# Chunked opening of a two-layer transformer trunk: x and the first weights by 128 contraction rows, bias lines made later and sent by GpSimd

## The chip, the cores and the metric

One of the eight cores of a Trainium2 chip runs the kernel. The metric is the device time of one execution in microseconds; the median of several runs is compared. A profiled execution gives the trace from which all rows here are taken. Engines: PE is TensorE (products), DVE is VectorE, ACT is ScalarE, POOL is GpSimd, SP is SyncE, which only issues DMAs here. ACT and POOL issue DMAs too.

## The reference

```python
# x: (1, 256, 1024) float32; one self layer, one cross layer
def diff_attention(x, w_in, lam_p, subln_g, w_out, rel_bias, lam_init):
    qkv = x @ w_in                      # 1024 -> 1024 Q, 1024 K, 1024 V
    ...                                 # 8 heads of two maps, dh 64, dv 128
    s = einsum('bqhmd,bkhmd->bhmqk', q_blk, k) + rel_bias[rel_bucket(rel)]
    p = softmax(where(rel >= 0, s, -inf))
    a = p[:, :, 0] - lam * p[:, :, 1]
    o = rms_norm(a @ v) * subln_g * (1 - lam_init)
    return o @ w_out

def reference(x, ...):
    h = layer_norm(ALPHA * x + diff_attention(x, ...))
    h = layer_norm(ALPHA * h + square(relu(h @ w_up[0])) @ w_down[0])
    h = layer_norm(ALPHA * h + moba_attention(h, w_q_b, w_out_b, shared_kv(h), rel_bias))
    return layer_norm(ALPHA * h + square(relu(h @ w_up[1])) @ w_down[1])
```

All of it is float32. The logits of both layers get a bias from one table of 32 buckets by 16 heads, chosen by the distance of query and key.

## The kernel before, in words

Every product of a projection is made as three passes: both operands are split into a float32r part (hi) and the rest (lo), and hi*hi, hi*lo and lo*hi accumulate in PSUM. `split_to` does this for a block: ACT copies the hi part, VectorE subtracts it to get lo.

The weights come in 96 units of 1 MB, in the order of their use. A unit is loaded in two pieces of 512 KB (`fetch`, on SP's queue) into five buffers named `raw`; `head` makes a piece's hi half on ACT, `piece` its lo half on VectorE, and then issues the load of the piece five further on, which needs that buffer. `bg` calls `piece` between products, by a credit that products earn. The split halves stand in seven buffers `whi` and `wlo`. From `attention(0, 0)` on every engine runs its instructions in the order of the program; each queue is in order, and a DMA issue that has to wait holds up all that is behind it on its engine. [...]

The opening is written out apart. The transposed x arrives in four parts of 256 KB (two chunks of 128 contraction rows each, all 256 tokens), and with each part two blocks of 256 KB of the first two units. `v_first(u)` (L377) handles a unit of V's first half of columns in two steps j of two chunks: split x (`split_x`), split the weights, the hi*hi products of both chunks and both halves of the tokens, then the lo products. After the first hi*hi products `make_lines` (L186) multiplies the table by a one-hot matrix, which gives one line of 384 biases per head; VectorE copies the lines out of PSUM. Products are 128 rows by 512 columns; V's accumulate in two PSUM banks over the eight chunks. `warm` is a bank for products of zeros ahead of the first real one.

`copy_lines` (L190) writes lines to DRAM (`scr`), 32 copies of each, by one DMA: heads 0 to 3 after `v_first(0)`, heads 4 to 15 after the first `bg`. Both are on ACT's queue. `load_bias` (L194) reads tiles of 128 queries by 256 keys back with four DMAs on SP's queue; the first pair's reads wait for the first copy, the second copy waits for those reads, and the second pair's reads (at i = 2 of the loop) wait for the second copy.

After V's first half, the loop over i (L616) projects Q and K of one pair of heads per round (`project`, 48 products of 256 columns), makes the halves of the pair before (`halves_hi` on ACT, `halves_lo` on VectorE), runs the softmax of the one before that, and multiplies the scores (`scores`, L478 to L480: first q hi by k hi, then q hi by k lo). `make_lambda` comes at i = 1; its two loads are on GpSimd's queue, which has had little else ahead of them.

Of the kernel before, what the change touches and what calls it, by code (L numbers as in the profile page):

```python
"""Differential-attention layer, squared-ReLU MLP, MoBA layer, squared-ReLU MLP, on one core.

Every float32 product of the projections runs as three float32r passes: both operands are
split exactly into a float32r part (11 mantissa bits) and the float32r rest, and
hi*hi + hi*lo + lo*hi accumulate in float32 in PSUM.  Scores are made the same way; the
products of the attention maps with V run as plain float32.

The sequence is one MoBA block, so no block lies in any query's past: the gate masks every
selected block, for all inputs, and the cross layer's softmax is over the own block.
"""  # L10
# [10 lines left out]
F32 = mybir.dt.float32  # L21
# [7 lines left out]
P = 128  # L29
D = 1024  # L30
S = 256
DEPTH = 2
NK = D // P
# [20 lines left out]
def trunk(ctx: ExitStack, tc: tile.TileContext, x, xT, units, lam_a, subln, rel_bias,  # L54
# [13 lines left out]
    def split_to(hi, lo, src, scale=None):  # L68
        """hi + lo = scale * src, both float32r."""
# [13 lines left out]
    def fetch(q):  # L83
        """Piece q's load."""
        if q < NU * PER:
            v, s = divmod(q, PER)
            raws[q] = wpool.tile([P, PIECE], F32, name="raw", bufs=RAWS)
            nc.sync.dma_start(raws[q], units[v][:, s * PIECE:(s + 1) * PIECE])

    def head():  # L90
        """The hi half of the next piece."""
# [13 lines left out]
    def piece():  # L105
        """The lo half of the next piece, after the hi half of a later one."""
# [12 lines left out]
    def bg(most=8, force=False):  # L119
        """Pieces of later units, as many as the products since the last ones have room for."""  # L120
# [7 lines left out]
    def unit(u, **dims):  # L128
        """The halves of unit u; units that were used up before are free from here on."""
# [5 lines left out]
    def three(ps, w, a, moving_w, n, start, stop):  # L135
        """ps += the product of a unit's block and an activation's, both (hi, lo)."""
# [29 lines left out]
    for q in range(4):  # L166
        raws[q] = wpool.tile([P, PIECE], F32, name="raw", bufs=RAWS)
        c = slice(q * 512, (q + 1) * 512)
        nc.sync.dma_start(xTr[:, c], xT[:, c])
        for j in range(2):  # L170
            d = (q % 2) * PIECE + j * 512
            nc.sync.dma_start(raws[q][:, j * 512:(j + 1) * 512], units[q // 2][:, d:d + 512])
# [17 lines left out]
    def copy_lines(h0, h1):  # L190
        nc.scalar.dma_start(scr[:, h0:h1].rearrange("p h r -> h p r"),
                            line[h0:h1, None, :].to_broadcast([h1 - h0, COPIES, RELS]))

    def load_bias(layer, p):  # L194
        """The tiles of pair p's two heads."""
# [6 lines left out]
    def split_x(s):  # L202
        k = slice(2 * s, 2 * s + 2)
        src = xTr.rearrange("p (k t) -> p k t", k=NK)[:, k]
        split_to(act[0][:, k], act[1][:, k], src)

# [18 lines left out]
    def rsqrt(v, n, scale=1.0, eps=None, eng=nc.vector, fill=()):  # L225
        """1/sqrt(scale * v + eps) of v [P, n]: a guess from the bits, then two steps.

        The guess is taken at an eighth.  The first step is of the third order,
        y <- y * (15 - 10 z + 3 z * z) / 8 with z = v * y * y, the second one Newton's,
        y <- y * (3 - z) / 2; the factors are shared out so that each is one instruction.  # L230
        `fill`: independent instructions, to be put between the dependent ones."""
# [16 lines left out]
        def shifted(o, a, c, b):  # L248
            """o <- (a + c) * b."""
# [745 lines left out]
```

## Time and profile before

| | us |
|---|---|
| median of three runs | 621.1 |
| lowest, highest | 619.33, 625.88 |
| span of the profiled execution | 621.2 |
| TensorE busy in it | 603.8 |
| VectorE busy | 385.8 |
| ACT busy | 325.5 |
| GpSimd busy | 15.4 |

The span runs from the first to the last instruction of the profiled execution, and is that execution's own time as the profile gives it. Busy time counts an engine's own instructions, and not the issuing of DMAs. In the rows below a timeline line is: start in us, duration in us, engine, line of the code, operation, output<-inputs, shapes, count; in brackets the idle time of the engine before it and what ended that.

### The profile page before, as it was taken

The numbers are of one execution on the slowest core, as the hardware profiler recorded it, in microseconds if no ns is written. First come the engines' busy times: TensorE is split into PE (matmuls) and PEld (weight loads), VectorE is DVE, ScalarE is ACT, GpSimd is POOL, SyncE is SP. The second block draws the span as 40 slices with busy tenths as digits, with TensorE's granted clock in tenths as the row PEclk, the third lists the DMA queues.
The fourth block names the chain that finished last, engine by engine and source line by source line (L and its number), as shares of the span: only waits on it lengthen the run. The fifth ranks groups of instructions, "written<-read, shape, count | busy, mean of one in ns | idle before, by whom it ended". The sixth has DMA issues, their size and how long they took to land.

```text
span 621.2 us, 9556 instructions
## 1 busy us (share of the span) xinstructions
PE 603.8 (97%) x3674; PEld 533.2 (86%) x3674; DVE 385.8 (62%) x706; ACT 325.5 (52%) x556; POOL 15.4 (2%) x40
## 2 busy tenths in 40 slices
PE   8999999999999999999999999999999999999994
PEld 5998987888898899898889899988898898899883
DVE  5479888877634734653877577877767534544236
ACT  5477787447654754552346466462586654554200
POOL 2000011000000000000020000000000000000000
PEclk9999999999999999999999999999999999999998
DMA  8797684547666556556258655341588656553001
GB/s 298 226 312 233 199 257 153 187 169 238 200 222 221 177 197 238 194 178 204 68 165 286 205 157 170 103 143 60 166 303 267 216 179 207 177 181 103 1 0 69
DMA packets 36985, 113.86 MB, mean 183 GB/s; under 512 B 4603, under 2 KB 9756, under 8 KB 36940
## 3 DMA queue, kind: packets, MB, share of 16 engines
q1 hardware_dynamic: 35056, 108.02, 52.9%
q0 software_dynamic: 1264, 4.39, 2.1%
q10 hardware_dynamic: 620, 0.84, 0.4%
q8 instruction: 29, 0.48, 0.3%
q14 instruction: 16, 0.13, 0.1%
HBM read 111.40 MB, written 1.84 MB: 182 GB/s over the span
## 4 chain that ended last, share of the span: by engine, by line
PE 74%; issue 10%; DMA 7%; DVE 5%; ACT 2%; POOL 1%; SPq 0%; DVEq 0%; POOLq 0%; ACTq 0%
PE ps_a L140 11%; PE ps_a L139 11%; PE ps_a L141 11%; PE ps_b L143 9%; PE ps_b L145 9%; PE ps_b L144 9%; DMA raw<-in_units 5%; PE ps_b L141 3%; PE ps_b L139 3%; PE ps_b L140 3%; DVE wlo L113 2%; DMA bias<-scr 1%; ACT whi L101 1%; PE ps_c L288 1%; PE ps_c L533 1%
## 5 line engine op out<-in xcount | busy, mean ns | idle before, releaser
L113 DVE TENSOR_TENSOR wlo<-raw,whi 128x1024 fp32r<-128x1024 f32 x188 | 222.8, 1221 | 66.6 <-ACT whi L101 66.1
L101 ACT ACTIVATE whi<-raw 128x1024 fp32r<-128x1024 f32 x188 | 190.4, 1053 | 83.8 <-PE ps_a L141 49.7
L143 PE MATMUL ps_b<-act_hi,whi 128*128 128x256 f32 x640 | 182.4, 285 | 0.0
L145 PE MATMUL ps_b<-act_hi,wlo 128*128 128x256 f32 x640 | 180.2, 282 | 0.0
L144 PE MATMUL ps_b<-act_lo,whi 128*128 128x256 f32 x640 | 179.9, 281 | 0.0
L144 PEld LDWEIGHTS ps_b<-act_lo,whi 128*128 128x128 f32 x640 | 120.6, 188 | 0.6
L143 PEld LDWEIGHTS ps_b<-act_hi,whi 128*128 128x128 f32 x640 | 120.5, 188 | 0.6
L145 PEld LDWEIGHTS ps_b<-act_hi,wlo 128*128 128x128 f32 x640 | 120.5, 188 | 0.0
L139 PE MATMUL ps_a<-whi,h_hi 128*128 128x512 f32 x248 | 98.5, 397 | 0.0
L141 PE MATMUL ps_a<-whi,h_lo 128*128 128x512 f32 x248 | 98.3, 396 | 0.0
L140 PE MATMUL ps_a<-wlo,h_hi 128*128 128x512 f32 x248 | 98.3, 396 | 0.0
L72 DVE TENSOR_TENSOR h_lo<-sqr,h_hi 128x512 fp32r<-128x512 f32 x24 | 16.6, 692 | 80.5 <-ACT h_hi L70 80.5
L141 PEld LDWEIGHTS ps_a<-whi,h_lo 128*128 128x128 f32 x248 | 46.7, 188 | 11.3
L140 PEld LDWEIGHTS ps_a<-wlo,h_hi 128*128 128x128 f32 x248 | 46.8, 189 | 10.8
L139 PEld LDWEIGHTS ps_a<-whi,h_hi 128*128 128x128 f32 x248 | 46.7, 188 | 10.8
L762 ACT ACTIVATE relu<-ps_b 128x512 f32<-128x512 f32 x32 | 19.1, 596 | 67.1 <-PE ps_b L145 56.8
L500 ACT ACTIVATE t<-t,mx 128x256 f32<-128x256 f32 x64 | 28.4, 444 | 34.5 <-DVE mx L497 34.5
L139 PE MATMUL ps_b<-whi,act_hi 128*128 128x512 f32 x96 | 39.4, 410 | 0.4 <-ACT act_hi L70 0.4
L141 PE MATMUL ps_b<-whi,act_lo 128*128 128x512 f32 x96 | 38.0, 396 | 1.0 <-DVE act_lo L74 1.0
L140 PE MATMUL ps_b<-wlo,act_hi 128*128 128x512 f32 x96 | 37.9, 395 | 0.0
L139 PE MATMUL ps_a<-whi,act_hi 128*128 128x512 f32 x80 | 32.5, 407 | 0.0
L140 PE MATMUL ps_a<-wlo,act_hi 128*128 128x512 f32 x80 | 31.6, 395 | 0.0
(142 smaller groups left out, 628.4 us busy)
## 6 DMA issues: line engine op xcount, KB each, us to landing
raw<-in_units SPq DMA_DIRECT2D x188, 512.0 KB, 5.2
bias<-scr SPq DMA_DIRECT2D x64, 64.0 KB, 4.2
raw<-in_units SPq DMA_DIRECT2D x8, 256.0 KB, 5.3
lnp<-in_ln_g POOLq DMA_DIRECT2D x4, 512.0 KB, 4.3
lnp<-in_ln_b POOLq DMA_DIRECT2D x4, 512.0 KB, 4.9
xres<-in_xT SPq DMA_DIRECT2D x4, 256.0 KB, 5.2
xres<-in_x SPq DMA_DIRECT2D x1, 1024.0 KB
scr<-lnp ACTq DMA_DIRECT2D x1, 576.0 KB
```

Source lines behind the costliest of these rows:

```text
L72: nc.vector.tensor_tensor(lo, src, hi.bitcast(F32), op=ALU.subtract)
L101: nc.scalar.activation(split[v][0][:, c], raws[state["head"]], AF.Copy)
L113: nc.vector.tensor_tensor(split[v][1][:, c], raws.pop(state["piece"]), split[v][0][:, c].bitcast(F32), op=ALU.subtract)
L139: nc.tensor.matmul(ps, a[0], w[0], start=start, stop=False)
L140: nc.tensor.matmul(ps, a[0], w[1], start=False, stop=False)
L141: nc.tensor.matmul(ps, a[1], w[0], start=False, stop=stop)
L143: nc.tensor.matmul(ps, w[0], a[0], start=start, stop=False)
L144: nc.tensor.matmul(ps, w[0], a[1], start=False, stop=False)
L145: nc.tensor.matmul(ps, w[1], a[0], start=False, stop=stop)
L288: nc.tensor.transpose(pt[:, j * P:(j + 1) * P], src[:, j * P:(j + 1) * P], ident)
L500: nc.scalar.activation(t[:, m, s], t[:, m, s], AF.Exp, bias=mx[:, m, j:j + 1], accum_out=sm[:, m, j:j + 1])
L762: nc.scalar.activation(r, ps, AF.Relu)
```

## The change

The x loads become eight of one chunk each, every one followed by the weight block of the same chunk. `v_first` goes by single chunks: split x, split the weights, then hi*hi for both halves of the tokens, lo*hi for both and hi*lo for both. In chunks 0 and 1 a product of zeros of 128 columns stands between the hi*hi and the lo products. `make_lines` moves from behind the first hi*hi products to behind chunk 4. The first copy of the lines moves from between the two V units to behind both, and both copies are issued by GpSimd instead of ACT. Comment lines and docstrings are blank in the new file; from L167 on its lines move by up to three.

```diff
-    for q in range(4):
-        raws[q] = wpool.tile([P, PIECE], F32, name="raw", bufs=RAWS)
-        c = slice(q * 512, (q + 1) * 512)
-        nc.sync.dma_start(xTr[:, c], xT[:, c])
-        for j in range(2):
-            d = (q % 2) * PIECE + j * 512
-            nc.sync.dma_start(raws[q][:, j * 512:(j + 1) * 512], units[q // 2][:, d:d + 512])
+    for k in range(NK):
+        if k % 2 == 0:
+            raws[k // 2] = wpool.tile([P, PIECE], F32, name="raw", bufs=RAWS)
+        nc.sync.dma_start(xTr[:, k * S:(k + 1) * S], xT[:, k * S:(k + 1) * S])
+        nc.sync.dma_start(raws[k // 2][:, (k % 2) * 512:(k % 2 + 1) * 512],
+                          units[k // 4][:, (k % 4) * 512:(k % 4 + 1) * 512])
...
     def copy_lines(h0, h1):
-        nc.scalar.dma_start(scr[:, h0:h1].rearrange("p h r -> h p r"),
+        nc.gpsimd.dma_start(scr[:, h0:h1].rearrange("p h r -> h p r"),
...
-    def split_x(s):
-        k = slice(2 * s, 2 * s + 2)
-        src = xTr.rearrange("p (k t) -> p k t", k=NK)[:, k]
-        split_to(act[0][:, k], act[1][:, k], src)
+    def split_x(k):
+        split_to(act[0][:, k], act[1][:, k], xTr[:, k * S:(k + 1) * S])
...
-                for j in range(2):
-                    q = 2 * u + j
-                    ks = (2 * j, 2 * j + 1)
-                    split_x(q)
-                    for k in ks:
-                        split_to(hi[:, k], lo[:, k], raws[q][:, (k % 2) * 512:(k % 2 + 1) * 512])
-                    del raws[q]
-                    fetch(q + RAWS)
-                    for k in ks:
-                        for h in range(2):
-                            nc.tensor.matmul(pv[0, h], at(4 * u + k, h)[0], hi[:, k], start=u == k == 0, stop=False)
-                    if q == 0:
+                for k in range(4):
+                    q, kk = 2 * u + k // 2, 4 * u + k
+                    split_x(kk)
+                    split_to(hi[:, k], lo[:, k], raws[q][:, (k % 2) * 512:(k % 2 + 1) * 512])
+                    if k % 2:
+                        del raws[q]
+                        fetch(q + RAWS)
+                    a = [at(kk, h) for h in range(2)]
+                    for h in range(2):
+                        nc.tensor.matmul(pv[0, h], a[h][0], hi[:, k], start=kk == 0, stop=False)
+                    if kk < 2:
+                        nc.tensor.matmul(warm[:, :P], zero[:, :P], zero[:, :P], start=True, stop=True)
+                    for h in range(2):
+                        nc.tensor.matmul(pv[0, h], a[h][1], hi[:, k], start=False, stop=False)
+                    for h in range(2):
+                        nc.tensor.matmul(pv[0, h], a[h][0], lo[:, k], start=False, stop=kk == NK - 1)
+                    if kk == 4:
                         make_lines()
-                    for k in ks:
-                        for h in range(2):
-                            a = at(4 * u + k, h)
-                            nc.tensor.matmul(pv[0, h], a[1], hi[:, k], start=False, stop=False)
-                            nc.tensor.matmul(pv[0, h], a[0], lo[:, k], start=False, stop=u == 1 and k == 3)
...
                 v_first(0)
+                v_first(1)
                 copy_lines(0, 4)
-                v_first(1)
                 load_bias(0, 0)
```

## Rows read from the trace of the kernel before

**Rows 1.** The page's part 1: busy us (share of the span) and instructions.

```profile
PE 603.8 (97%) x3674; PEld 533.2 (86%) x3674; DVE 385.8 (62%) x706; ACT 325.5 (52%) x556; POOL 15.4 (2%) x40
```

**Rows 2.** Timeline of ACT and VectorE in the opening.

```profile
5.29 0.63 ACT L70 ACTIVATE whi<-raw 128x512 fp32r<-128x512 f32 x1 [0.32 <-DMA raw<-in_units]
...
9.87 0.55 DVE L188 COPY lnp<-ps_c 16x384 f32<-16x384 f32 x1 [1.98 <-PE ps_c L187]
...
10.45 0.28 ACTq L191 DMA_DIRECT2D scr<-lnp  x1
```

**Rows 3.** Timeline of TensorE in the opening.

```profile
5.98 2.46 PE L395 MATMUL ps_a<-whi,act_hi 128*128 128x512 f32 x4 [0.74 <-ACT whi L70]
8.37 1.46 PE L187 MATMUL ps_c<-lnp,table 33*16 33x384 f32 x2
9.76 0.79 PE L401 MATMUL ps_a<-whi,act_lo 128*128 128x512 f32 x1
...
12.06 0.63 PE L402 MATMUL ps_a<-wlo,act_hi 128*128 128x512 f32 x1
12.49 0.55 PE L401 MATMUL ps_a<-whi,act_lo 128*128 128x512 f32 x1
12.88 0.39 PE L402 MATMUL ps_a<-wlo,act_hi 128*128 128x512 f32 x1
...
21.01 0.40 PE L401 MATMUL ps_a<-whi,act_lo 128*128 128x512 f32 x1
21.24 0.40 PE L402 MATMUL ps_a<-wlo,act_hi 128*128 128x512 f32 x1
```

**Rows 4.** Windows: stretch, its length, busy us (count) by engine; PEclk, DMA share, GB/s.

```profile
4.00:13.00 9.00, 8.23 (x17) 4.16 (x17) 5.21 (x9) 5.99 (x11) 0.87 (x2) 1.00 1.01 355
```

**Rows 5.** Timeline of SP from 20 us on, issues of one line merged.

```profile
21.79 1.75 SPq L198 DMA_DIRECT2D bias<-scr  x4
23.64 13.38 SPq L88 DMA_DIRECT2D raw<-in_units  x8
38.64 1.74 SPq L198 DMA_DIRECT2D bias<-scr  x4
```

**Rows 6.** Waits of SP's queue up to 40 us: total, times, longest.

```profile
SPq L198 <- DMA scr<-lnp: 7.2, 2, 5.6
```

**Rows 7.** One link of the chain; VectorE's timeline at that place.

```profile
24.11 6.92 DMA raw<-in_units
...
23.07 1.23 DVE L113 TENSOR_TENSOR wlo<-raw,whi 128x1024 fp32r<-128x1024 f32 x1 [0.69 <-ACT whi L101]
```

**Rows 8.** Timeline of TensorE and VectorE at 33 and 48 us.

```profile
33.19 0.47 PE L478 MATMUL ps_a<-kz,qh 128*128 128x512 f32 x1
34.42 0.47 PE L479 MATMUL ps_a<-kz,qh 128*128 128x512 f32 x1 [0.76 <-DVE kz L468]
...
47.25 0.42 DVE L491 CUSTOM_DVE_ANT_0 t<-ps_a,bias 128x256 f32<-128x256 f32 x1 [2.33 <-DMA bias<-scr]
...
48.09 0.40 PE L478 MATMUL ps_a<-kz,qh 128*128 128x512 f32 x1
49.80 0.50 PE L479 MATMUL ps_a<-kz,qh 128*128 128x512 f32 x1 [1.31 <-DVE kz L468]
```

**Rows 9.** Bias tiles' landing up to 60 us; DMA issues up to 40 us.

```profile
DMA to landing us min/median/max: 2.2/4.8/6.4
...
lnp<-in_lam_a POOLq DMA_DIRECT2D x1, 128.0 KB, 5.9
ident<-in_ident POOLq DMA_DIRECT2D x1, 64.0 KB, 4.3
```

**Rows 10.** DMA queue of ACT, 14.1 to 21.3: packets, MB, share of 16 engines.

```profile
q10 hardware_dynamic: 131, 0.20, 7.4%
```

**Rows 11.** The same from 31 to 38.7 us.

```profile
q10 hardware_dynamic: 396, 0.59, 25.0%
```

**Rows 12.** Timeline of VectorE: the first instruction that reads lambda's load.

```profile
36.58 0.28 DVE L217 TENSOR_TENSOR lp<-lnp 128x128 f32<-128x128 f32 x1
```

## The prediction

> **What bounds the kernel now.** The page's busy times come first: TensorE is busy for 603.8 of 621.2 us [rows 1]. Past the opening the kernel is a row of products, so a change to the first 22 us can give two things: the time at which that row becomes gapless, and the waits that start-up loads cause a little later. TensorE's timeline has two such waits, at 33 and at 48 us, both for the low halves of keys that VectorE makes; they are read below. Nothing after about 50 us is touched.
>
> The opening is read from the timeline by engine. The first real product starts at 5.98, when ACT has the first weight chunk's high half (5.29 to 5.92) [rows 2, 3]. Four hi*hi products follow with gaps, then the lines' product at 8.37, and from there TensorE has no gap worth naming; the stage's last product starts at 21.24 and ends at 21.64 [rows 3]. [...] The windows view grants 1.00 in all of 4 to 13, so here the spacing has to be read instead [rows 3, 4].
>
> Two in-order queues lose time to the bias lines. VectorE waits 1.98 us for the lines' product before it copies them, and ACT issues their way to DRAM at 10.45 [rows 2]. SP then stands 5.6 us, from 16.2 to 21.79, because its first bias tiles read that copy; weight loads follow only at 23.64 [rows 5, 6].
>
> That hole returns later. The chain shows the load issued at 24.11 as one link of 6.92 us. It would put VectorE's low half ahead of it, but that one starts at 23.07, takes 1.23 us and ends at 24.30, after the issue: what set 24.11 is SP's order behind the bias tiles [rows 7]. The load lands at 31.03; ACT splits it, makes the halves of pair 0 behind it, VectorE the low ones, and TensorE, which started the scores at 33.19, goes on at 34.42 [rows 8]. The wait from 48.09 to 49.80 goes back to bias tiles too: VectorE stands until 47.25 for tiles that SP issued at 38.64 [rows 5, 8].
>
> **Loads in chunks.** The bytes are the same: eight x loads of 128 KB for four of 256 KB, the weights as before. That is four more issues of about 0.44 us on SP (1.75 for four [rows 5]), at most 1.8 us, and it delays the last chunk most; by 355 GB/s [rows 4] 384 KB take 1.1 us, so that chunk lands near 13.5 and TensorE comes to it after 18 (below). I take nothing; without that cover it would be the 1.8. The first weight chunk has 128 KB less in front of it, 0.4 us at that rate. First product: 5.98 - 0.43 = 5.55, at worst 5.98.
>
> **Splitting and products by chunk.** A chunk costs ACT 0.63 for the weights [rows 2] and some 0.35 for x, VectorE about 0.65 and 0.35 (from 1.23 for 1024 columns [rows 7], estimates): 1.0 each, less than the loads' 1.1. [...]
>
> When the clock rises is the disputed cost. It rose 4.5 us after 8.37 and 3.1 us after 9.76, from where the spacing is even; before 8.37 there are gaps of up to 0.74 us [rows 3]. I take 4.5, as 8.37 opens the last stretch without a gap: 10.05. The ends are 3.1 (8.7) and no earlier than now (12.9). [...]
>
> With 10.05: (10.05 - 5.55)/0.43 = 10.5 products are done, 42.5 x 0.232 = 9.9 remain, end 19.9. Then the lines: their product stands behind chunk 4 now, and VectorE's copy of them ahead of chunk 5's low halves. TensorE is through the lines (35 of the 53) at 10.05 + 24.5 x 0.232 = 15.7, the copy (0.55 [rows 2]) ends at 16.3, and chunk 5's products with low halves wait about 0.5 for x and 0.15 for the weights. V ends at 20.55 instead of 21.64: **-1.1 us**, between -1.7 (8.7) and +0.2 (12.9).
>
> VectorE, which would be through chunk 4 near 11, stands until then. Chunks 5 to 7 end on it at 19.3, and the four pieces behind (1.23 each) at 20.6 to 24.3. The first Q/K unit wants its low half at 20.8: just covered. Two weight loads that wait for chunks 5 and 7 issue at 17.3 and 19.4, where the last was out by 16.2; they fall into the hole in the loads.
>
> **The lines' copy on GpSimd.** It is issued at 16.3 instead of 10.45. How long 192 KB take there is not shown. From below: a bias load at its best, 2.2 us [rows 9], so 18.5. From above: as long as on ACT, 10.45 to 21.79 = 11.3, so 27.6. But all of that copy's packets (128 rows) moved in 14.1 to 21.3, for 7.4% of the engines' time [rows 10], among weight loads; at 17 to 20 there are one or two of those. The nearest rows are GpSimd's own loads of 64 and 128 KB, 4.3 and 5.9 us in the crowded opening [rows 9]; I take 4.5: SP is free at 20.8, 1.0 earlier. [...]
>
> The loads behind SP then come 1.0 earlier: 31.03 becomes 30.0. Against that, the second copy (576 KB, waits for the first bias tiles' landing as it did on ACT) starts near 25.5, where on ACT it moved in 31 to 38.7 for 25.0% of the engines' time [rows 11]. A quarter of three us is +0.75. So TensorE resumes at 34.2 instead of 34.42, though it would be ready at 32.3: of the 1.1 us **-0.25 us** is left; the rest goes into a longer wait. Ends: -2.1 (TensorE's own order, copy in 2.2 us) and +5.8.
>
> The second pair's bias tiles wait for the second copy. If that takes 8 us, between 5.9 for 128 KB [rows 9] and the rest of the present one, it lands near 33.5; then SP's own order decides, just after its last load is out, 37.0 - 0.25 = 36.8 instead of 38.64 [rows 5]. Of 1.85 us, 1.5 can be used, since TensorE's wait is 1.71 less a product's 0.23 [rows 8]: **-1.3 us**, bounds 0 (the tiles queue behind weight loads whenever they are issued) and -1.5.
>
> The loads for lambda now queue behind both copies on GpSimd: issued near 26.5, behind the second copy's packets, landing at 33 to 35.5. VectorE wants them at 36.58 [rows 12]. Taken as nothing; each us beyond costs VectorE one.
>
> Sum: -0.25 - 1.3 = -1.55; 621.2 - 1.55 = 619.6. The profiled span, 621.2, stands at the median of the three runs, 621.1.
>
> **Rivals.** *Gain lost* (0.2): the copies on GpSimd bring the bias tiles no earlier, TensorE arrives sooner and waits longer at 33 and 48: 621.2. For it: 34.42 is set by loads, not by products. Against: SP's 5.6 us. If chunks land no sooner than now, that is 0.4 us of V's gain and ends here too.
> *Slower* (0.15): the first copy, made 5.9 us later than now, lands later than now. Its place is SP's queue, where every weight load waits. It decides from 5.5 us on (21.8); with the second copy's gain counted, the kernel is slower from 6.8. With 11.3 us SP is free 5.8 late: 627.0; midway, 8 to 9 us, 623 to 624.
> *Both stages gain* (0.15): clock at 8.7, copies near 2.2 us. V -1.7, the waits of 1.0 and 1.5 gone: -4.2, 617.0.
>
> **How the numbers follow.** Forecast 0.5, alone 618.2 to 620.8. The range runs from the large gain with 0.2 for the spread of its terms, 616.8, to the middle of the slow rival, 623.5; it leaves out some 0.08 on either side. One per cent is 6.2 us, about what a measurement of this kernel can tell from no change. No sum reaches -6.2 but by errors in several terms (0.04); the slow rival reaches +6.2 only at its end with some loss besides (0.05); the rest, 0.91, lies within.
>
> **What would show it.** First V product near 5.55; spacing 0.23 from 8.7 to 12.9 on; VectorE waiting 4 to 5 us for the lines' product, copy done near 16.3; V's end near 20.55; SP's first bias issue near 20.8; TensorE resuming the scores at about 34.2; the second pair's tiles issued near 36.8 and the wait at 48 nearly gone. I am wrong if SP's bias issue comes after 21.8, if GpSimd's copy moves at ACT's pace, or if VectorE's late pieces, not loads, hold TensorE at 20 to 26.

## The result and the profile after

The changed kernel takes 626.4 us (median of 20 runs, 624.43 to 630.04) against 621.83 (20 runs of the kernel before beside them, 618.95 to 625.88). The ratio is 1.0077, interval 1.0059 to 1.0095: 0.8% slower, where a gain of 0.25% was forecast, and outside the range.

The page's part 1 of the changed kernel, as in [rows 1], shows hardly more work on any engine (GpSimd 17.1 us against 15.4); TensorE is busy for 603.4 us against 603.8, in a span of 623.7 against 621.2. The loss is idle time.

```profile
PE 603.4 (97%) x3678; PEld 533.3 (86%) x3678; DVE 386.5 (62%) x710; ACT 325.8 (52%) x560; POOL 17.1 (3%) x42
```

TensorE's timeline of the changed kernel, to be read beside [rows 3] and [rows 8]: the V stage starts at 5.71 and runs at 0.23 us per product nearly from its start (two products take from 6.97 to 7.43), so it is through at 19.30 (18.66 + 0.64), 2.3 us ahead of before. Then come two waits of 3.28 and 0.76 us ahead of the first scores, which end 1.9 us behind before (36.33 against 34.42), and one of 1.69 at the third pair's scores, which ends 4.35 behind (54.15 against 49.80).

```profile
5.71 0.74 PE L391 MATMUL ps_a<-whi,act_hi 128*128 128x512 f32 x2 [0.47 <-ACT whi L70]
...
6.97 0.62 PE L397 MATMUL ps_a<-wlo,act_hi 128*128 128x512 f32 x2
7.43 0.68 PE L391 MATMUL ps_a<-whi,act_hi 128*128 128x512 f32 x2
...
18.66 0.64 PE L397 MATMUL ps_a<-wlo,act_hi 128*128 128x512 f32 x2
...
35.11 0.47 PE L475 MATMUL ps_a<-kz,qh 128*128 128x512 f32 x1 [3.28 <-ACT kz L455]
36.33 0.77 PE L476 MATMUL ps_a<-kz,qh 128*128 128x512 f32 x1 [0.76 <-DVE kz L465]
...
54.15 0.50 PE L476 MATMUL ps_a<-kz,qh 128*128 128x512 f32 x1 [1.69 <-DVE kz L465]
```

Where this comes from is read off four queues. VectorE's timeline has the copy of the lines out of PSUM, the first lambda instruction, and the softmax of the first and the second pair (`t<-ps_a,bias`):

```profile
14.23 0.55 DVE L187 COPY lnp<-ps_c 16x384 f32<-16x384 f32 x1 [2.40 <-PE ps_c L186]
...
41.15 0.29 DVE L214 TENSOR_TENSOR lp<-lnp 128x128 f32<-128x128 f32 x1 [2.57 <-DMA lnp<-in_lam_a]
...
42.28 0.42 DVE L488 CUSTOM_DVE_ANT_0 t<-ps_a,bias 128x256 f32<-128x256 f32 x1
...
51.60 0.43 DVE L488 CUSTOM_DVE_ANT_0 t<-ps_a,bias 128x256 f32<-128x256 f32 x1 [1.90 <-DMA bias<-scr]
```

GpSimd's timeline has the two copies and the lambda load, SP's the bias tiles:

```profile
15.09 0.77 POOL L190 DMA_DIRECT2D scr<-lnp  x1 [11.20 <-DVE lnp L187]
28.91 0.69 POOL L190 DMA_DIRECT2D scr<-lnp  x1 [13.06 <-DMA bias<-scr]
29.60 0.62 POOL L210 DMA_DIRECT2D lnp<-in_lam_a  x1
```

```profile
24.91 1.75 SPq L197 DMA_DIRECT2D bias<-scr  x4
26.76 12.46 SPq L88 DMA_DIRECT2D raw<-in_units  x8
40.52 1.74 SPq L197 DMA_DIRECT2D bias<-scr  x4
```

These rows are one serial chain: lines, first copy, first bias tiles, second copy (its issue waits for those tiles, as the bracket of 28.91 says), second bias tiles, second pair's softmax. Link by link, before [rows 2, 5, 8] and after; the second copy of before is this line of ACT's timeline:

```profile
26.56 0.32 ACTq L191 DMA_DIRECT2D scr<-lnp  x1
```

| step | before | after | link is longer by |
|---|---|---|---|
| lines copied from | 9.87 | 14.23 | +4.36 |
| first copy issued | 10.45 | 15.09 | +0.28 |
| SP issues first bias tiles | 21.79 | 24.91 | -1.52 |
| second copy issued | 26.56 | 28.91 | -0.77 |
| SP issues second bias tiles | 38.64 | 40.52 | -0.47 |
| second pair's softmax starts | 47.25 | 51.60 | +2.47 |

From the lines to that softmax both kernels take 37.4 us, though single links differ by up to 2.5 us and only cancel in the sum. The lines are made 4.36 us later, the softmax comes 4.35 later, and the median is 4.57 later. That coincidence of sums is a reading; the experiments test it.

The two spans differ by less, 2.5 us, but the rest is not made up in the opening. From the second softmax on both kernels run the same instructions on VectorE, and matched one by one the changed kernel is 4.4 us behind still at 145 us. Past that the kernel before waited more in this execution: its last 2900 products take 476.9 us from start to start, the changed kernel's 475.4. This execution lay above its median: in the nineteen other profiled ones the device time is 1.8 to 2.2 us above the span, which puts this one near 623.1, about 1.3 above 621.83 (an estimate from those figures).

### The profile page after: what moved, and what is told of

Read it like the earlier page. It is cut to its first block, busy times and chain, and to the rows that moved or that the text cites. A ratio compares the mean times of both kernels' runs of the same rounds, so it can differ in the third digit from the quotient of the medians.

```text
span 623.7 us, 9580 instructions
## 1 busy us (share of the span) xinstructions
PE 603.4 (97%) x3678; PEld 533.3 (86%) x3678; DVE 386.5 (62%) x710; ACT 325.8 (52%) x560; POOL 17.1 (3%) x42
## 4 chain that ended last, share of the span: by engine, by line
PE 75%; issue 10%; DMA 8%; DVE 4%; ACT 2%; POOL 1%; SPq 1%; DVEq 0%; POOLq 0%; ACTq 0%
PE ps_a L140 11%; PE ps_a L141 11%; PE ps_a L139 11%; PE ps_b L143 9%; PE ps_b L145 9%; PE ps_b L144 9%; PE ps_b L141 3%; PE ps_b L139 3%; PE ps_b L140 3%; DMA raw<-in_units 3%; DMA lnp<-in_lam_a 2%; DVE wlo L113 2%; DMA scr<-lnp 2%; DMA bias<-scr 1%; PE ps_c L285 1%
## 5 line engine op out<-in xcount | busy, mean ns | idle before, releaser
L141 PEld LDWEIGHTS ps_a<-whi,h_lo 128*128 128x128 f32 x248 | 46.7, 188 | 11.3
L140 PEld LDWEIGHTS ps_a<-wlo,h_hi 128*128 128x128 f32 x248 | 46.8, 189 | 10.8
L139 PEld LDWEIGHTS ps_a<-whi,h_hi 128*128 128x128 f32 x248 | 46.7, 188 | 10.8
L141 PE MATMUL ps_a<-whi,act_lo 128*128 128x512 f32 x80 | 31.6, 395 | 0.0
## 6 DMA issues: line engine op xcount, KB each, us to landing
scr<-lnp POOLq DMA_DIRECT2D x1, 576.0 KB, 11.6
```

Source lines behind the costliest of these rows:

```text
L139: nc.tensor.matmul(ps, a[0], w[0], start=start, stop=False)
L140: nc.tensor.matmul(ps, a[0], w[1], start=False, stop=False)
L141: nc.tensor.matmul(ps, a[1], w[0], start=False, stop=stop)
```

## The experiments

All are timed in five rounds beside the kernel before, on its chip. A profile is one execution, and the profiled ones lay up to some 3 us from their kernel's own median, so ratios are taken from all runs and places from the profile.

| kernel | lines | copy 1 | bias 1 | copy 2 | bias 2 | softmax 2 | span | profiled time less median | ratio |
|---|---|---|---|---|---|---|---|---|---|
| before | 9.87 | 10.45 | 21.79 | 26.56 | 38.64 | 47.25 | 621.2 | about +1.3 | 1 |
| after | 14.23 | 15.09 | 24.91 | 28.91 | 40.52 | 51.60 | 623.7 | -0.8 | 1.0077 |
| e1 | 15.38 | 15.96 | 25.20 | 29.03 | 42.46 | 50.28 | 624.4 | 0.0 | 1.0074 |
| e2 | 8.48 | 9.33 | 19.84 | 25.74 | 36.94 | 46.65 | 619.6 | -2.4 | 1.0042 |
| e3 | 14.37 | 14.95 | 24.01 | 28.51 | 39.64 | 48.58 | 624.1 | +1.7 | 1.0051 |
| e4 | 15.08 | 15.93 | 26.08 | 29.57 | 41.88 | 50.50 | 623.5 | -0.2 | 1.0071 |
| e5 | 10.47 | 11.32 | 21.75 | 26.82 | 38.25 | 47.69 | 621.3 | -2.8 | 1.0068 |
| e6 | 15.71 | 16.29 | 25.33 | 28.71 | 40.86 | 49.48 | 624.2 | +1.5 | 1.0039 |
| e7 | 15.19 | 16.05 | 24.04 | 28.00 | 37.73 | 46.76 | 617.3 | -0.9 | 0.9965 |
| e8 | 9.77 | 11.15 | 21.44 | 25.90 | 39.66 | 48.94 | 618.4 | +0.9 | 0.9952 |
| e9 | 10.64 | 11.21 | 21.11 | 28.25 | 38.00 | 50.50 | 625.5 | +2.4 | 1.0069 |
| e10 | 15.60 | 16.45 | 25.81 | 29.71 | 41.39 | 50.62 | 625.2 | +0.3 | 1.0083 |
| e11 | 14.76 | 15.61 | 25.46 | 29.43 | 41.39 | 50.80 | 625.2 | +0.2 | 1.0094 |
| e12 | 12.57 | 13.15 | 23.10 | 27.75 | 39.82 | 48.25 | 620.5 | +0.3 | 0.9989 |
| e13 | 16.51 | 17.36 | 27.19 | 31.09 | 42.61 | 51.85 | 625.3 | +0.2 | 1.0113 |
| e14 | 11.71 | 12.28 | 23.34 | 30.17 | 40.69 | 50.49 | 622.8 | +0.3 | 1.0056 |
| e15 | 16.57 | 17.42 | 27.28 | 31.28 | 42.88 | 54.03 | 626.1 | +1.3 | 1.0089 |
| e16 | 11.98 | 12.56 | 18.56 | 25.72 | 35.79 | 43.50 | 614.5 | -3.0 | 0.9983 |
| e17 | 17.02 | 17.87 | 27.99 | 35.52 | 46.06 | 55.18 | 630.3 | +0.6 | 1.0132 |
| e18 | 12.32 | 12.90 | 18.86 | 28.31 | 37.08 | 47.23 | 620.7 | 0.0 | 1.0027 |

The columns are the steps of the chain above, in us. Over the 20 rows the span goes with the start of the second softmax: correlation 0.90, 1.2 us of span per us (least squares); without the five kernels with spread lines (e7, e8, e12, e16, e18), whose products are quicker all through (below), 0.89 and 0.96. The link to the lines is looser: e6's lines come 5.84 us behind before's, its second softmax 2.23. And the chain has a second end. In eight profiles (e2, e3, e5, e7, e10, e11, e13, e17) the second softmax waits for no bias tile; it follows the first one at 7.2 to 7.5 us, and the first one stood behind the lambda load, for which VectorE waited 0.9 to 8.7 us and which lies behind the second copy on GpSimd. So the second softmax is a good sign of an execution's length; what causes it rests on the edits below that move the chain on purpose.

**e1 to e4: who issues the copies.** e1, e3 and e4 give both copies, the first, or the second of the changed kernel back to ACT; e2 gives both copies of the kernel before to GpSimd.

```diff
     def copy_lines(h0, h1):
-        nc.gpsimd.dma_start(scr[:, h0:h1].rearrange("p h r -> h p r"),
+        nc.scalar.dma_start(scr[:, h0:h1].rearrange("p h r -> h p r"),
```

> The changed kernel with both copies of the lines issued by ACT again; all else as changed. Theory 1 (GpSimd's copies hold SP and share the weight loads' engines): the whole loss goes, SP's first bias issue comes before 22 us although the lines are made near 14.5, and the time is 618.5 to 622 (ratio to before 0.995 to 1.000). Theory 2 (the lines are made too late, whoever sends them): SP is freed no earlier than about 24, and the time stays at 624 to 627.

> The kernel before with both copies issued by GpSimd; loads, products and lines as before. Theory 1: the first copy takes 9 to 10 us from 10.5 and lands near 20 to 22, the second takes 11 to 12 us and slows weight loads and lambda's loads behind it; the time is 1 to 4 us above before (ratio 1.002 to 1.006). Theory 2: the lines are as early as before, so the time is that of before within 0.2 per cent.

> The changed kernel with only the first copy (heads 0 to 3) issued by ACT, the second still by GpSimd. Theory 1, if the first copy's hold on SP is what costs: SP freed before 22, time 619 to 622.5. If the second copy and lambda's loads behind it cost most: 623 to 626. Theory 2: 624 to 627.

> The changed kernel with only the second copy (heads 4 to 15) issued by ACT, the first still by GpSimd. Theory 1 with the first copy as the cause: SP still freed near 25, time 624 to 627. With the second copy as the cause: 619 to 622.5. Theory 2: 624 to 627.

Measured: e1 1.0074 (1.0046 to 1.0103), e3 1.0051 (1.0028 to 1.0073), e4 1.0071 (1.0039 to 1.0103), e2 1.0042 (1.0020 to 1.0064). From its issue to SP's bias issue the first copy takes 9.2 us on ACT in e1 and 9.1 in e3, 10.5 on GpSimd in e2 and 9.8 in the changed kernel. The theory that GpSimd's way of issuing is the cause falls: with ACT the loss stays. e1's queue rows:

```profile
15.96 0.27 ACTq L190 DMA_DIRECT2D scr<-lnp  x1
...
25.20 1.75 SPq L197 DMA_DIRECT2D bias<-scr  x4
```

GpSimd costs something where all else is as before (e2), and there the lambda load lies behind the second copy, so that the first softmax waits for it and starts at 39.42 and not at 37.71; but with the chunks in place its share is not to be told from nothing. VectorE's timeline of e2:

```profile
38.28 0.29 DVE L217 TENSOR_TENSOR lp<-lnp 128x128 f32<-128x128 f32 x1 [4.24 <-DMA lnp<-in_lam_a]
```

**e5, e6, e9, e10: the parts alone and by twos.** e5 is the changed kernel with lines and first copy behind chunk 1; e6 the kernel before with the lines made behind its third step (`if q == 2`) and the first copy behind both V units; e9 the changed kernel with lines early, first copy between the units and ACT issuing, so that only the chunks remain; e10 is e6 with GpSimd issuing.

```diff
 e5, e9:
-                    if kk == 4:
+                    if kk == 1:
                         make_lines()
 e6, e10:
-                    if q == 0:
+                    if q == 2:
                         make_lines()
```

> The changed kernel with the lines made after chunk 1 (not 4) and the first copy issued by GpSimd right behind them. Theory 2 (the copy takes 9 to 11 us from whoever sends it, so what counts is when the lines are made): the copy is issued near 10, SP is freed near 20 to 21, the wait before the first scores shrinks below 1.5 us; time 619 to 622.5 (ratio 0.997 to 1.002). Theory 3 (chunk loads or the products' new order cost the time): it stays at 624 to 627.

> The kernel before, its loads, splits and products by pairs of chunks as before and both copies on ACT, with the lines made behind the hi*hi products of chunks 4 and 5 and the first copy behind both V units. Theory 2: SP is freed 3 to 5 us later than before, near 25 to 27; time 624 to 627. Theory 3: within 0.2 per cent of before.

> The chunks alone: lines made behind chunk 1 and their first copy sent between the two units, both copies by ScalarE as before; only the order of loads, splits and products is the changed kernel's. Theory A (the chunks themselves cost, since the V projection that ends 1 to 2 us earlier is only a longer wait for the weight and bias loads, after which TensorE's clock is halved): ratio 1.002 to 1.004, a wait of over 3 us on TensorE ahead of the first scores and a granted clock near 0.5 behind it. Theory B (the chunks cost nothing by themselves; the late lines and GpSimd's copies are all of it): ratio 0.997 to 1.001, no wait over 3 us.

> The two other parts without the chunks: the kernel before with its lines made behind the first unit's third quarter, the first copy sent behind both units, and both copies by GpSimd. If the late place (+0.39% alone) and GpSimd (+0.42% alone) add up: ratio 1.007 to 1.009, as much as the whole change. If they cost the same thing once (the first copy, 9 to 11 us long by either issuer, lies beside the same weight loads): 1.003 to 1.005, and the chunks' share of the change is the rest, some 0.3 to 0.4%.

Measured: e5 1.0068 (1.0037 to 1.0100), e6 1.0039 (1.0010 to 1.0068), e9 1.0069 (1.0041 to 1.0098), e10 1.0083 (1.0053 to 1.0112). With c for the chunks, l for the late lines and g for GpSimd the eight combinations are, in per cent: none 0, c 0.69, l 0.39, g 0.42, cl 0.74, cg 0.68, lg 0.83, clg 0.77. Without the chunks l and g add up; with them neither adds anything that can be measured. Each part alone makes the kernel slower, and the whole costs no more than the chunks alone, as far as these figures tell (each is uncertain by some 0.3). In e5 and e9 SP issues the first bias tiles at 21.75 and 21.11, no later than before, and the loss is there all the same: the late first copy is one cause and not the only one.

That the chunks cost, though V ends sooner, was the surprise. Neither expectation for e9 was met: the ratio lies above both ranges, and TensorE does not wait ahead of the first scores. In e9's profile V is through at 19.88 (19.25 + 0.63), and TensorE then waits for weights and runs on at half pace, as its timeline shows; in the window from 20 to 25 us the granted clock is 0.73:

```profile
19.25 0.63 PE L397 MATMUL ps_a<-wlo,act_hi 128*128 128x512 f32 x2
20.69 0.39 PE L143 MATMUL ps_b<-act_hi,whi 128*128 128x256 f32 x1 [0.81 <-ACT whi L101]
...
21.95 0.38 PE L145 MATMUL ps_b<-act_hi,wlo 128*128 128x256 f32 x1 [0.76 <-DVE wlo L113]
```

And the first bias tiles, issued at 21.11, free the second copy only at 28.25: 7.1 us, against 4.8 in the kernel before. There the stretch from 20 to 25 us is nearly empty, with 0.31 of the DMA engines busy, since SP has stood behind the copy; here the weight loads that were issued later run in it, at 0.93. The second softmax is at 50.50, 3.25 us behind before. This profile lay 2.4 us above its median, so the size may be too large. That this is how the chunks cost is a reading of one profile, and no edit tests it.

**e14, e13: loads by chunks or products by chunks.** e14 gives the kernel before the 16 loads of the changed kernel and leaves all else; e13 gives the changed kernel the 12 loads of before.

```diff
 e14 (e13 is the reverse, in the changed kernel)
-    for q in range(4):
-        ...
-        nc.sync.dma_start(xTr[:, c], xT[:, c])
+    for k in range(NK):
+        ...
+        nc.sync.dma_start(xTr[:, k * S:(k + 1) * S], xT[:, k * S:(k + 1) * S])
```

> The kernel before with the changed kernel's 16 loads at the start; it splits and multiplies by quarters as before, lines early, copies by ScalarE. Theory L: the load behind the V units starts a us later or more, less moved by 30 us than 7.90 MB, ratio 1.003 to 1.007, most of what the chunks cost alone (1.0069). Theory N, and the theory that it is the product order by chunks that costs: ratio 0.998 to 1.001.

> The changed kernel with x loaded by quarters of two chunks again (12 loads at the start in place of 16); split and multiplied by chunks, late lines and GpSimd as changed. Theory L (16 loads hold the load queue longer, so that the load behind the V units starts 1 us later, 9.85 against 8.89, and 1.1 MB less has been moved by 30 us, which TensorE then waits for): that load starts before 9.0 us, the sum moved by 30 us rises by 0.3 MB or more, ratio 1.002 to 1.006. Theory N (the loads' size doesn't matter; with late lines the first copy and what waits for it is all): ratio 1.007 to 1.009 as changed, and under 7.0 MB by 30 us.

Measured: e14 1.0056 (1.0027 to 1.0085), which looks like most of what the chunks cost. In SP's timeline of e14 the loads of the later units start at 12.77, where before had 8.89 in the same view, and the first bias tiles, issued at 23.34, take 6.8 us until the second copy leaves at 30.17.

```profile
12.13 0.43 SPq L170 DMA_DIRECT2D raw<-in_units  x1
12.77 10.51 SPq L88 DMA_DIRECT2D raw<-in_units  x5
23.34 1.83 SPq L197 DMA_DIRECT2D bias<-scr  x4
```

But the loads are not alone in that delay. e14 splits x by pairs of chunks, so its first split waits for the second chunk of x, which now comes behind the first weights. In this kernel alone ACT's table load, 1.28 us long and through by 3.6 us in all the others, stands behind that wait. The first V product starts at 8.21 (before: 5.98), and V ends 3.2 us behind before's. ACT's and TensorE's timelines of e14:

```profile
5.71 1.28 ACT L70 ACT_TABLE_LOAD   x1 [5.71 <-DMA xres<-in_xT]
...
8.21 2.07 PE L394 MATMUL ps_a<-whi,act_hi 128*128 128x512 f32 x4 [2.97 <-ACT whi L70]
```

So its 0.56% is not the price of the loads alone.

e13 came out the other way than that theory asked: 1.0113 (1.0070 to 1.0155), no better than the changed kernel, though its later loads start at 8.32. Its lines come at 16.51, 2.3 us behind the changed kernel's, because VectorE waits 4.54 us for their product behind chunk 4, and the chain ends at 51.85. TensorE went through the first chunks at half pace in that execution (the two products at 7.16 take 1.20 us, where the changed kernel's take 0.71), so part of these 2.3 us may be its clock's. No run shows that loads by chunks cost anything where the splits go by chunks too: with loads by quarters e13 is no faster than the changed kernel, and e16 (below) no faster than e12.

**e7, e8, e12: lines spread over more partitions.** The first copy reads four lines, which lie on partitions 0 to 3. Theory 4 is that the copies are paced by the partitions that they read from. Here head h's line stands on partition 4h; a table of 64 columns, used in every fourth, puts it there. Everything else is as changed (e7), as before (e8), or as in e9 (e12).

```diff
-    table = const.tile([NBUCKET + 1, NH], F32, name="table")
+    table = const.tile([NBUCKET + 1, 4 * NH], F32, name="table")
...
-    nc.scalar.dma_start(table[:NBUCKET], rel_bias)
+    nc.scalar.dma_start(table[:NBUCKET, ::4], rel_bias)
...
-                            line[h0:h1, None, :].to_broadcast([h1 - h0, COPIES, RELS]))
+                            line[4 * h0:4 * h1:4, None, :].to_broadcast([h1 - h0, COPIES, RELS]))
```

> The changed kernel with the line of head h on partition 4h instead of h (the one-hot product makes 64 rows, three of four unused); bytes, packets, issuers and order as changed. [...] If the count of DMA engines or the writing to DRAM sets the pace: SP freed near 25, time 624 to 627.

> The kernel before with the line of head h on partition 4h; all else as before. Theory 4: the first copy, issued near 10.5 on ACT, lands by 17 instead of 21.8, SP no longer waits for it longer than for its own buffers, and the waits at 33 and 48 shrink; time 617 to 620.5. If not: that of before within 0.2 per cent.

> The chunks with lines early, copies by ScalarE, and the lines of the 16 heads on every fourth partition. Theory 4 (the copies are paced by the partitions that they read from): second copy under 9.5 us, lambda loads landed a us or two earlier; ratio 0.993 to 0.998, no slower than the spread lines with the changed order (0.9965). If the chunks cost what theory A says, it stays above the kernel before with spread lines (0.9952); if they cost nothing, it is the fastest of all, 0.993 to 0.995.

Measured: e7 0.9965 (0.9933 to 0.9996), e8 0.9952 (0.9922 to 0.9982), e12 0.9989 (0.9956 to 1.0022). The same edit takes 1.1% off the changed kernel and 0.8% off e9; e7 and e8 are faster than the kernel before, the only ones whose interval says so, though e7's lines are as late as ever. The copies fell short of theory 4, though: e7's still takes 8.0 us, against 9.8 in the changed kernel, and e8's is through at 21.44 and not by 17. That e8's time fell into the expected range is in part luck, as follows. The DMA view by queue, from 15 to 25 us of the changed kernel and from 16 to 24.1 of e7 (packets, MB, share of 16 engines), shows the first copy as q0 with the same packets and bytes:

```profile
q1 hardware_dynamic: 556, 2.00, 51.6%
q0 software_dynamic: 192, 0.20, 16.3%
```

```profile
q1 hardware_dynamic: 673, 2.41, 75.4%
q0 software_dynamic: 192, 0.20, 6.9%
```

0.163 x 16 x 10 us is 26 us of engine time in the one, 0.069 x 16 x 8.1 is 9 us in the other; the weights beside it move faster too. In the kernel before [rows 10], where the copy went out earlier among more weight loads, its packets took 0.074 x 16 x 7.2 = 8.5 us, no more than spread ones. The lines' copy takes 8.0 us in place of 9.8 and the second 9.7 in place of 11.6 (issue to the next issue), and the second softmax moves from 51.60 to 46.76, ahead of before, and waits for no bias tile:

```profile
46.76 0.42 DVE L488 CUSTOM_DVE_ANT_0 t<-ps_a,bias 128x256 f32<-128x256 f32 x1
```

In e8 the chain shows no gain: the copies take 10.3 and 13.8 us there, and the second softmax, at 48.94, waits 4.84 us for the bias, more than before. What made e8 faster lies outside the opening: matched by VectorE's instructions it is 3.6 us behind before at 145 us still, and its span is 2.8 us shorter. In all five kernels with spread lines TensorE's products follow each other more quickly through the whole kernel: the last 2900 of them, counted from start to start without gaps over 0.5 us, take 469.1 to 470.8 us, where the fifteen others need 473.4 to 474.0 (before 473.6, e8 470.3, e7 470.8). A product of 256 columns comes every 117 ns there and every 119 elsewhere (medians). Part 1 of the pages of e8 and e7, to be read beside [rows 1]:

```profile
PE 598.3 (97%) x3674; PEld 530.8 (86%) x3674; DVE 386.6 (63%) x706; ACT 326.0 (53%) x556; POOL 15.4 (2%) x40
```

```profile
PE 598.7 (97%) x3678; PEld 531.1 (86%) x3678; DVE 386.7 (63%) x710; ACT 325.4 (53%) x560; POOL 17.0 (3%) x42
```

For e8 that is 3.3 us, as much as its whole gain of 0.48%; for e7 it is 2.8 us, 0.45%. No wait in the opening explains it. The edit also makes `table` four times as wide, and no run has that alone, so its cause is open. What is left for the copies is some 0.7% between e7 and the changed kernel, where the second softmax shows it, 0.4% between e12 and e9, and nothing between e8 and before.

**e11: the clock behind the long wait.** After the wait of 3.28 us the changed kernel's products run at half pace; the window from 36 to 39.5 us has a granted clock of 0.51 (the kernel before: 1.00), and its products of 256 columns start 0.21 us apart, against 0.12 from 39.58 on. e11 fills the wait with products of zeros whose output is not used.

```diff
                 qh, ql = Q.pop(p)
+                if layer == 0 and p == 0:
+                    for _ in range(7):
+                        nc.tensor.matmul(warm[:, :256], zero[:, :P], zero[:, :256], start=True, stop=True)
```

> The changed kernel with seven products of zeros (128 by 256, output unused) on TensorE ahead of the first scores, where it waited 3.28 us and ran at half clock afterwards; all else as changed. Theory A1 (the fall of the clock behind that wait is a large part of the loss): the granted clock stays near 1 to 44 us, the scores and projections between 36 and 39.5 us run at full pace, and the ratio falls by 0.2 to 0.3% to 1.004 to 1.006. Theory A2 (what is late are the loads, bias and lambda behind the copies, and TensorE has to wait for them anyway): the clock stays up and the time doesn't move, 1.007 to 1.008, with the next wait longer by as much.

The windows of the changed kernel and of e11 (stretch, length, busy us by engine, granted clock, DMA share, GB/s), and TensorE's timeline of e11:

```profile
36.00:39.50 3.50, 3.17 (x13) 3.01 (x14) 2.54 (x3) 0.04 (x1) 0.00 (x0) 0.51 0.85 171
```

```profile
36.00:39.50 3.50, 3.38 (x26) 3.32 (x27) 2.36 (x2) 0.00 (x0) 0.00 (x0) 1.00 0.88 174
```

```profile
32.16 3.18 PE L472 MATMUL ps_c<-lnp 128*128 128x256 f32 x14
34.99 0.58 PE L478 MATMUL ps_a<-kz,qh 128*128 128x512 f32 x1
...
44.29 0.47 PE L478 MATMUL ps_a<-kz,qh 128*128 128x512 f32 x1 [1.42 <-ACT kz L455]
```

The clock stays up and twice as many products fit into the window (26 against 13), but the time doesn't fall: 1.0094 (1.0058 to 1.0131). TensorE is early at the second pair's scores and waits for them; their softmax is at 50.80. So no part of the loss is shown to be the clock's, though the test is not clean: VectorE waits 3.86 us for the lambda load in e11's profile, and from 100 to 116 us the granted clock is 0.89 there and 1.00 in the changed kernel's.

**e15: the lambda loads.** The changed kernel with the two loads sent by GpSimd at the start, ahead of both copies.

> The changed kernel with the two lambda loads sent by GpSimd at the start, ahead of both copies, where the changed kernel sent them behind the second copy (landed at 41.12, and VectorE waited 2.57 us for them). If that wait is on the path: lp runs by 37 us, no wait for it on VectorE, ratio down by 0.2 to 0.4% to 1.004 to 1.006. If VectorE's wait is beside TensorE's for bias and weights: 1.007 to 1.009.

1.0089 (1.0054 to 1.0125). VectorE no longer waits for the load, but the test is not clean: the load lies beside the first weights now, TensorE is at half pace up to 10.7 us, the lines come at 16.57 instead of 14.23, and the chain ends at 54.03. e1, where ACT issues the copies and lambda's loads have nothing ahead of them, is the cleaner sign: its first softmax starts at 39.36, 2.9 us ahead of the changed kernel's, and the loss is the same (1.0074).

**e16 to e18: out of the load queue.** e16 is e12 with loads by quarters. e17 (of the changed kernel) and e18 (of e16) send the first bias tiles from GpSimd, so that weight loads on SP don't stand behind the copy.

```diff
-                load_bias(0, 0)
+                load_bias(0, 0, nc.gpsimd)
```

> Chunks of split and product alone, with loads by quarters, lines early and spread over every fourth partition, copies by ScalarE. Theory L: faster than the same with 16 loads (0.9989), 0.992 to 0.997, and level with or ahead of the kernel before with spread lines (0.9952). Theory N: 0.998 to 1.001 as with 16 loads.

> The changed kernel with the first bias load (four DMAs) sent by GpSimd, behind its own first copy, in place of SyncE; SyncE goes on with weight loads and doesn't stand behind the copy from 17.94 to 24.91 us. Theory Q (the standing load queue is what costs: weights come later, TensorE waits for them): a weight load is issued between 18 and 24 us, the data moved by 46 us rises from 11.75 MB by 0.5 MB or more, ratio 0.998 to 1.003. Theory B (the bias itself is what TensorE waits for, by way of the softmax): no gain, 1.006 to 1.010, with the same waits ahead of the first scores.

> The kernel with chunks of split and product, loads by quarters, lines early and spread, copies by ScalarE (0.9983), with the first bias load sent by GpSimd. Theory Q: 0.990 to 0.996, the fastest of all. Theory B: 0.996 to 1.000, as without it.

e16: 0.9983 (0.9950 to 1.0016), not to be told from e12. Its first copy takes 6.0 us, as e18's, the shortest of all, and its profile, 3 us under its own median, the shortest span. e17: 1.0132 (1.0088 to 1.0177); e18: 1.0027 (0.9998 to 1.0056). They give no support to the theory that the standing load queue costs, but don't refute it, since weights did not come sooner: by 46 us e17 had moved 10.8 MB, the changed kernel 11.7 (the last figure of the rows, GB/s, times 46 us; the changed kernel first):

```profile
0.00:46.00 46.00, 38.53 (x218) 32.32 (x219) 24.13 (x47) 23.83 (x44) 6.53 (x15) 0.96 0.82 255
```

```profile
0.00:46.00 46.00, 37.65 (x212) 31.55 (x212) 19.58 (x30) 19.98 (x31) 7.56 (x17) 0.99 0.82 235
```

In e17 SP sends weights without a break, the tiles land later among them, so the second copy leaves at 35.52 instead of 28.91, and the lambda load behind it holds VectorE for 8.73 us and TensorE for 6.28. VectorE's and TensorE's timelines of e17:

```profile
46.33 0.29 DVE L214 TENSOR_TENSOR lp<-lnp 128x128 f32<-128x128 f32 x1 [8.73 <-DMA lnp<-in_lam_a]
```

```profile
48.39 0.76 PE L475 MATMUL ps_a<-kz,qh 128*128 128x512 f32 x1 [6.28 <-ACT kz L455]
```

So weight loads sent past the tiles cost more than they gave, since tiles, second copy and lambda load came later. SP's order, which kept weights behind the tiles, had kept the way clear for them. What weights that really come sooner would be worth, no run shows.

## Why the prediction was wrong

**The step that failed** is "I take 4.5: SP is free at 20.8, 1.0 earlier". The first copy took 9.8 us and SP was free at 24.91, 3.1 later than before. The price was taken from GpSimd's loads of 64 and 128 KB, which end on all partitions, while the copy starts from four. It takes 9.0 to 10.5 us, issue to bias issue, in thirteen of the fourteen kernels with unspread lines other than before, late or early and with either issuer, and 11.3 before (in e14 SP came to the tiles too late to tell). The prediction's own rows [rows 10] had 0.20 MB in 7.2 us, 28 GB/s, which was read as a copy waiting among weight loads, since it used 7.4% of the engines' time. For the kernel before that may hold: e8's spread copy is hardly quicker. What failed is the step from there to a quick copy once the weight loads thin out: in the changed kernel the same bytes held the engines for 26 us. The slow rival, at 0.15, was the case: it was to decide from 5.5 us of copy, and its prices (623 to 624 at 8 to 9 us, 627.0 at 11.3) enclose the measured loss of 4.6 us. Another issuer left the copy nearly as long as it was: 9.2 us in e1 and 9.1 in e3, from ACT, against 9.8 from GpSimd.

**The same size is missed in the second copy**: 8 us taken, 11.6 measured; with the later start the second tiles are issued at 40.52 and not at 36.8. The 1.3 us that this was to give became 2.47 lost in the tiles' own landing, and the wait at 48 [rows 8] stayed, at 52, with 1.69 us.

**The lambda loads, "taken as nothing"**, landed at 41.13 (29.60 + 11.53 by the chain) instead of 33 to 35.5, and VectorE waited 2.57 us. e17 shows that such a wait reaches TensorE; in the changed kernel it lies beside the late second tiles, and e1 and e4, whose lambda loads do not lie behind the second copy, lose as much, so its share there is not told from nothing.

**What was right.** First product 5.71 (5.55 forecast). The clock: full pace in the first two chunks instead of at 10.05, ahead of the bounds (the sum's 0.43 and 0.232 us per product are the starts of [rows 3], 12.06 to 12.49 and 21.01 to 21.24); so V gained 2.3 us and not 1.1, the lines were copied by 14.78 and not 16.3, and all of it was lost again as its first rival said ("TensorE arrives sooner and waits longer"). The clock was luck of the execution: e17 has the same V stage and reaches full pace at 11.2, and of the fourteen profiles with splits by chunks eight reach full pace at 6.7 to 7.7 us, and six only at 10.3 to 11.2, with V's end at 21.1 to 22.1. That an earlier V stage is worth little held by the wait of 3.28 us. In the sum's count of 53 products no row of before shows the price of the two extra ones, taken as one each, nor that the 53 follow each other without a gap. In the changed kernel a chunk with an extra product took 1.67 us (7.43 to 9.10) and the next one, without, 1.39 (to 10.49): 0.28 us, 1.2 products of 0.232. The lines, taken as three, took 0.75 (13.38 to 14.13), 3.2 products, and one gap was 0.32 us (ahead of 15.17).

**What was left out** is that the chunks have a price. The prediction gave them a small gain ("-0.25 us is left"); alone they cost 0.69% (e9), with SP at its bias tiles as early as before. Which part of them costs is not shown: the loads, "I take nothing", bring a loss in e14 only together with a V stage that starts 2.2 us late, and leaving them out of e13 and e16 gains nothing. The prediction also set a profiled span, 621.2, beside a median of device times, 621.1; that execution itself took about 2 us more.

**What stays open**: why spread lines make products quicker in the whole kernel; what in the chunks costs; why e2 and e5 are slower by 0.42 and 0.68% with a second softmax within 0.6 us of before in their profiles (both profiles lay over 2 us under their medians, so the usual execution was not seen); and the shares of the three parts in the changed kernel, as they don't add.

## What to carry to other kernels

Write a start-up out as the serial chain of everything that one DMA's landing lets go, through DRAM and back, with all its ends, and price each link by its own row. Don't expect the end to move as the start does: 4.4 us and 4.4 in the changed kernel, 5.8 and 2.2 in e6. Don't price a DMA by a load of the same size from other partitions, nor by its share of the engines' time in another place: compare the time that the same packets take (the first copy's: 8.5 us of the engines' time before, 26 in the changed kernel, 9 in e7). When a faster stage ends in a wait, ask which chain ends that wait before counting the gain. And when an edit helps, see where in the trace: a large part of what spread lines gave lay past the opening that they were meant for.

## What the runs showed of the hardware

In the changed kernel the copy from four neighbouring partitions keeps its slow pace when the other traffic thins out. From 21.1 to 24.4 us the DMA view shows 0.08 MB of it, 24 GB/s, and 0.10 MB of weights, with the engines busy for a quarter of the time. Below is the view from 19 to 25 us in 40 slices of 0.15 us, the fifteenth at 21.1. A packet counts in the slice where it starts: a slice of 31 is one packet of the copy, one of 27 a packet of weights, so that no single slice is a rate.

```profile
GB/s 219 249 300 358 335 300 304 300 382 304 225 164 113 164 85 61 27 31 27 85 61 27 31 27 85 61 27 31 27 85 51 27 48 55 102 102 109 109 109 109
```

In e7 the same 192 packets used a third of the engine time from the partitions 0, 4, 8 and 12: 9 us against 26. The place of the lines does not set the pace alone: in the kernel before, from partitions 0 to 3, the copy's packets used 8.5 us, no more than e7's, and spread copies still took 6.0 to 10.3 us among weight loads. What makes them slow, no run shows.

The weights came late too: in the changed kernel VectorE waited 5.12 us for the high half of a piece that was loaded beside the first copy.

```profile
26.20 2.56 DVE L113 TENSOR_TENSOR wlo<-raw,whi 128x1024 fp32r<-128x1024 f32 x2 [5.12 <-ACT whi L101]
```

And TensorE's clock can fall to half behind one wait (0.51 behind the 3.28 us of the changed kernel) and be kept at 1.00 by products of zeros in it (e11), without a gain in time that the runs show.
